# A two-layer decoder trunk on one core: chunk 2 of the SwiGLU FFN in seven block products, and norm steps issued ahead of weight splits

## The chip, the core and the metric

The kernel runs on one core of one Trainium2 chip. The time is device microseconds of one execution. Before the change it is 641.0 us, the median of 3 runs (639.06 to 641.35 us). One further execution was taken with the hardware profiler on; all rows below come from that one.

## The reference

Two layers, each a token mixer and a SwiGLU FFN, both between RMSNorms, on x of 256 rows by 1024 columns, all in float32:

```
h = h + rmsnorm(mixer(rmsnorm(h, mix_pre_norm)), mix_post_norm)
f = (silu(n @ w_gate) * (n @ w_up)) @ w_down      # n = rmsnorm(h, ffn_pre_norm)
h = h + rmsnorm(f, ffn_post_norm)
```

The mixer projects n by w_in (1024 x 3088) into attention heads and gated-linear-attention heads, and its result goes through w_out (1024 x 1024). w_gate and w_up are 1024 x 2816 and w_down is 2816 x 1024. The change touches the FFN and the norms between mixer and FFN; the mixer's inside is as it was.

## The kernel before, in words

**Three products for one.** Each float32 operand is split into a high part (`hi`, rounded to the float32r type by a ScalarE copy) and a low part (`lo`, the difference, by a VectorE subtraction). A product is then three TensorE matmuls: hi by hi, hi by lo, lo by hi. Weights come from HBM in pieces of two 128-row tiles by 512 columns (128x1024 in the rows), so each piece costs one ScalarE copy (`wh<-...`) and one VectorE subtraction (`wl<-...`). `highs` (L417) issues the copies and `lows_` (L437) the subtractions, both strictly in the order of `queue`. The split pieces lie in a ring of NW = 8: piece i can be split only when the matmuls on piece i-8 are done for both halves of the rows (j = 0 and j = 1, 128 rows each).

**The FFN's chunks.** The 2816 hidden columns go in six chunks, five of 512 and one of 256 (`FF_CHUNKS`). A plain chunk multiplies both row halves by w_gate and w_up: 8 row tiles of weight, two matrices, two halves, three matmuls, 96 matmuls of 128x512, and 8 weight pieces. A chunk listed in `SEVEN` (L42) goes through `seven` (L1283) instead: the 2x2 block product (two row halves by {gate, up}, with the 1024 inner rows cut in two) is computed with seven block products in place of eight: 84 matmuls. Its seven weight blocks (`SNAMES`) are three loaded ones and four sums (v1 to v4) of loaded ones; each block is two pieces, so 14 copies, 14 subtractions, and 8 additions of 128x1024 on VectorE for the sums (`sums`, L375). The results are combined by five small 128x512 VectorE operations (`gate0`, `hidden`) where a plain chunk has two. After chunk c, `down` (L1350) multiplies chunk c-1 by its 512 rows of w_down: four weight pieces, 48 matmuls for both halves.

**Tiles and loads.** Plain pieces are loaded into a ring of four (`raw`, NRAW). A seven-product chunk takes five tiles of 1 MB out of NBIG = 8 (`b11`, `b12`, `v1`, `b22`, `b21`; v2 and v4 are formed in b11's place, v3 in b12's). From the start of the FFN to the end of chunk 4 two more of the eight hold the split sums of the activations. All loads are issued by SyncE in one order (`loader`, L355).

**The order of the work.** `Clock` (L108) is a planner that runs when the program is built: it keeps an estimated time for each engine and wakes tasks by it. PE's estimated time is "now". `lows_` issues a subtraction when VectorE's estimated end is less than 0.7 us ahead of now; `sums` issues an addition when VectorE is not ahead at all, or up to 0.7 us when its block is due within two pieces. Each engine then executes its instructions in that order, waiting at each for its inputs. A step of a norm waits for `soon(x)` (L252), the estimated time at which x is ready, and is issued then; weight splits issued before that stand in front of it.

**The norms.** `post_norm` (L673) squares and sums the two PSUM banks of a row half (`sq`, ScalarE), multiplies by the gain (`pn`, VectorE), forms the factor (`var` on VectorE, `rstd` on GpSimd), and adds to h. `pre_norm_ffn` (L592) squares h, scales it (`xn`), transposes it on PE (`tp_x`), scales by the gain column (`a`), and splits (`xh_x` on ScalarE, `xl_x` on VectorE). Chunk 1's first product (`b11`, in the bank `seven_a`) is the first user of that.

Of the kernel before, what the change touches and what calls it, by code (L numbers as in the profile page):

```python
# [38 lines left out]
NEG = -1e30  # L39
LEVELS = (16, 8, 4, 2, 1)  # L40
FF_CHUNKS = (512, 512, 512, 512, 512, 256)
SEVEN = (1, 3, 4)  # L42
SNAMES = ("b11", "b21", "v2", "v1", "v3", "b22", "v4")
NW = 8
NRAW = 4
# [6 lines left out]
UNITS1 = [("gqk", 0), ("aq", 0), ("gqk", 1), ("aq", 1)] + UNITS0[2:]  # L52
BANKS = {"mm": 2, "tp": 2, "ac": 4}
SEM = 0.2


class Engine:
# [50 lines left out]
class Clock:  # L108
# [40 lines left out]
    def note(self, eng, cost, ins, outs):  # L149
# [3 lines left out]
        for ap in ins:  # L153
            r = self.ready(ap)
            start = max(start, r if eng == "PE" and ap in outs else r + SEM)
        if eng == "DMA":
# [21 lines left out]
    def tile(self, pool, shape, dtype, tag, bufs, name):  # L178
# [3 lines left out]
        while len(slots) >= bufs:  # L182
            done = [t for t in slots if t not in self.open]
            if done:
                t = min(done, key=lambda t: self.last.get(t, 0.0))
                slots.remove(t)
                free = self.last.get(t, 0.0) + SEM
                yield free
# [8 lines left out]
    def close(self, *tiles):  # L197
        for t in tiles:
            self.open.discard(t.tensor.name)

    def after(self, new, old):

        self.free[new.tensor.name] = self.last.get(old.tensor.name, 0.0) + SEM

# [33 lines left out]
def trunk(ctx: ExitStack, tc: tile.TileContext, io: dict):  # L238
# [7 lines left out]
    ck = Clock(nc)  # L246
    pe, act, dve, pool, dma, close = ck.pe, ck.act, ck.dve, ck.pool, ck.dma, ck.close

    def at(*aps):
        return ck.ready(*aps) + 0.5  # L250

    def soon(*aps):  # L252

        return ck.ready(*aps)

    def bank(tag, name):
        t = yield from ck.tile(ps, [P, 512], F32, tag, BANKS[tag], name)
        ck.port[t.tensor.name] = ("", 0.0)
        return t

    def t2(name):
        return ck.tile(sb, [P, 512], F32, "t2", NT2, name)
# [4 lines left out]
    def small(name, n=1):  # L267
        return sb.tile([P, n], F32, tag="small", bufs=20, name=name)
# [18 lines left out]
    def add_seven(l, c, f0, fw, what="all"):  # L287

        blocks = {}
        for n, name in ((1, "w_gate"), (2, "w_up")):  # L290
            for k in range(2):
                blocks[f"b{k + 1}{n}"] = io[name][l][512 * k:512 * (k + 1), f0:f0 + fw]
        if what != "rest":
            forms[l, c] = {"tiles": {}, "ready": {}, "low": {}}
        for name in {"first": ("b11", "b21"), "rest": ("b12", "v1", "b22")}.get(
                what, ("b11", "b12", "v1", "b22", "b21")):
            loads.append((name, (l, c), blocks.get(name)))
        for name in {"first": SNAMES[:2], "rest": SNAMES[2:]}.get(what, SNAMES):
            for g in range(2):
                queue.append(((l, "seven", c, name), 2 * g, 2, fw, None))  # L300

    for l in range(L):
# [10 lines left out]
        for c, fw in enumerate(FF_CHUNKS):  # L313
            if c == 0:
                add_seven(l, 1, fw, FF_CHUNKS[1], "first")
            if c in SEVEN:
                add_seven(l, c, f0, fw, "all" if c > 1 else "rest")
# [210 lines left out]
    def load_gain(i):  # L528
        if i < len(gains):
            gtiles[i] = gain(gains[i], D, "gain", 1)  # L530


    def rstd_of(parts_, n):

        v = small("var", n)
        if len(parts_) == 1:
            dve.tensor_scalar(v, parts_[0], EPS, None, op0=ALU.add)
        else:
            dve.scalar_tensor_tensor(v, parts_[0], EPS, parts_[1], op0=ALU.add, op1=ALU.add)
        r = small("rstd", n)  # L540
        pool.tensor_tensor(r, v, nhalf[:, :n], op=ALU.pow)
        return r

    def transpose_pe(src, t0, m, tp):
        for i in range(m):
            pe.transpose(tp[:, i * P:(i + 1) * P], src[:, (t0 + i) * P:(t0 + i + 1) * P], ident)
        return tp.rearrange("p (k t) -> p k t", t=P)[:, :m, :]
# [44 lines left out]
    def pre_norm_ffn(j, out, l):  # L592


        ms = []
        for i in range(2):
            c = slice(i * 512, (i + 1) * 512)
            junk = yield from ck.tile(sb, [P, 512], BF16, "t2", NT2, "sq")
            yield soon(h[j][:, c])
            m = small("ms")  # L600
            act.activation(junk, h[j][:, c], AF.Square, scale=1.0 / 32.0, accum_out=m)
            close(junk)
            ms.append(m)
        yield soon(*ms)
        r = rstd_of(ms, 1)
        xs = []
        if j == 0:
            sums_of[l] = []
            for name, dtype in (("a", F32), ("sums_h", R32), ("sums_l", R32)):
                t = yield from ck.tile(sb, [P, 4, 512], dtype, "big", NBIG, name)  # L610
                sums_of[l].append(t)
        while len(sums_of[l]) < 3:
            yield ck.now() + 0.1
        a = sums_of[l][0]
        for i in range(2):
            c = slice(i * 512, (i + 1) * 512)
            x = yield from t2("xn")
            yield soon(r)
            act.activation(x, h[j][:, c], AF.Copy, scale=r)
            xs.append(x)  # L620
        xt = []
        for i in range(2):
            hi = yield from ck.tile(sb, [P, 4, P], R32, f"xt{j}", 6, "xh_x")
            lo = yield from ck.tile(sb, [P, 4, P], R32, f"xt{j}", 6, "xl_x")
            yield at(xs[i])
            tp = yield from bank("tp", "tp_x")
            tv = transpose_pe(xs[i], 0, 4, tp)
            close(xs[i])
            yield soon(tp)
            av = a[:, 2 * j + i, :]  # L630
            for k in range(4):
                g = 16 + 8 * l + 4 * i + k
                act.activation(av[:, k * P:(k + 1) * P], tv[:, k, :], AF.Copy, scale=gcol[:, g:g + 1])
            close(tp)
            yield soon(av)
            act.activation(hi.rearrange("p k t -> p (k t)"), av, AF.Copy)
            yield soon(hi)
            dve.tensor_tensor(lo.rearrange("p k t -> p (k t)"), av,
                              hi.rearrange("p k t -> p (k t)").bitcast(F32), op=ALU.subtract)
            xt += [(hi[:, k, :], lo[:, k, :]) for k in range(4)]  # L640
        out[j] = xt
        if j == 1:
            yield from sums_x(out, l)
# [29 lines left out]
    def post_norm(j, banks, gi, then):  # L673

        g = gtiles[gi]
        ms, ts = [], []

        def square(i):
            junk = yield from t2("sq")
            yield soon(banks[i])  # L680
            m = small("msh")
            act.activation(junk, banks[i], AF.Square, scale=1.0 / 32.0, accum_out=m)
            close(junk)
            ms.append(m)

        def gained(i):
            t = yield from t2("pn")
            yield ck.port[banks[i].tensor.name][1]
            dve.tensor_tensor(t, banks[i], g[:, i * 512:(i + 1) * 512], op=ALU.mult)
            close(banks[i])  # L690
            ts.append(t)

        yield from square(0)
        if ck.ready(banks[1]) <= ck.at["Act"]:
            yield from square(1)
            yield from gained(0)
        else:
            yield from gained(0)
            yield from square(1)
        yield soon(*ms)  # L700
        r = rstd_of(ms, 1)
        yield from gained(1)
        yield soon(r)
        for i, w in ((0, 512), (512, 256), (768, 256)) if j and then is None else ((0, 512), (512, 512)):
            c = slice(i, i + w)
            dve.scalar_tensor_tensor(h[j][:, c], ts[i // 512][:, i % 512:i % 512 + w], r, h[j][:, c],
                                     op0=ALU.mult, op1=ALU.add)
            if then is None:
                dma.dma_start(io["out"][0, j * P:(j + 1) * P, c], h[j][:, c])
        close(*ts)  # L710
        if j == 1:
            load_gain(gi + 1)
        if then is not None:
            yield from then


    def mixer(l, xin, xout):
# [482 lines left out]
        for j in range(2):  # L1200
            while mixed[j][4] is None:
                yield ck.now() + 0.2
            bk = []
            for i in range(2):
                o = yield from bank("ac", f"wo{i}")
                bk.append(o)
            for part, lo in (("wo_g", 4), ("wo_a", 0)):
                while mixed[j][lo] is None:
                    yield ck.now() + 0.2
                yield from project((l, part), mixed[j][lo:lo + 4], bk, first=(lo == 4),  # L1210
                                   last=(lo == 0))
                close_x(mixed[j][lo:lo + 4])
            go(post_norm(j, bk, gi, pre_norm_ffn(j, xout, l)))


    def ffn(l, xin, xout):
# [145 lines left out]
        for c in range(nch):  # L1362
            if c in SEVEN:
                seq = []
# [5 lines left out]
            for part, j in seq:  # L1370
                yield from part(c, j)
            if c == max(SEVEN):
                close(*xin[2]["tiles"])
# [30 lines left out]
    h = [const.tile([P, D], F32, name=f"h{j}") for j in range(2)]  # L1404
# [110 lines left out]
```

## Time and profile before

| what | value |
|---|---|
| median of 3 runs | 641.0 us (639.06 to 641.35) |
| the profiled execution's own time | 639.99 us |
| its span, first to last instruction | 638.2 us |
| mean granted TensorE clock | 0.989 of full |
| mean HBM read rate over the span | 170 GB/s |
| VectorE instructions / ScalarE instructions | 784 / 700 |

How to read it: a busy share is an average over stages with different limits, so what a stage is worth is read from the stage's own window. PE is TensorE's matmuls, PEld its weight loads, DVE is VectorE, ACT is ScalarE, POOL is GpSimd, SP is SyncE. The duration of a matmul is that of a pipeline, longer than the distance from one matmul to the next. All instructions are recorded on L77, the helper that issues them, so they are told apart by the names of their tiles.

In layer 0 the FFN runs from 135.7 us to 323 us (first and last of its matmuls), in layer 1 from 447.7 us to 631.5 us.

### The profile page before, as it was taken

The page shows a single profiled execution, that of the slowest core. Times are in us where ns is not written, and L with a number is a line of the kernel's source. Part 1 is how long each engine was busy: PE and PEld are TensorE (multiplying, and loading weights), DVE is VectorE, ACT ScalarE, POOL GpSimd, SP SyncE. Part 2 cuts the span into 40 slices and gives each one's busy share as a digit, 9 for nine tenths or more (in the row PEclk, how much of TensorE's full clock was granted, in tenths as well). Part 3 has the DMA queues.
Part 4 walks back from the last instruction along what each step waited for, and adds up shares of the span by engine and source line. Part 5 has one row for each costly group of instructions (what it writes and reads, how often), then busy time and mean ns, then how long its engine had stood idle before and what let it go on. Part 6 is the DMA issues. An engine that isn't in the chain of part 4 may idle for free.

```text
span 638.2 us, 10255 instructions
## 1 busy us (share of the span) xinstructions
PE 622.1 (97%) x3896; PEld 510.7 (80%) x3896; DVE 504.3 (79%) x784; ACT 412.6 (65%) x700; POOL 23.7 (4%) x41
## 2 busy tenths in 40 slices
PE   8999999989999999999999999999899999999995
PEld 7987778868888888879788777887788888888894
DVE  4899975579897899987588996557899778989743
ACT  6889855486946385656577797537966555838531
POOL 1000021000000000000010000110000000000000
PEclk9999999979999999999999999999899999999998
DMA  8965455156048946039474714840910895710811
GB/s 281 281 193 156 149 188 191 52 174 255 1 142 294 397 152 201 1 104 289 142 246 149 205 46 126 277 142 17 368 45 3 286 353 216 270 61 1 263 68 66
DMA packets 53108, 109.30 MB, mean 171 GB/s; under 512 B 5890, under 2 KB 10692, under 8 KB 53060
## 3 DMA queue, kind: packets, MB, share of 16 engines
q1 hardware_dynamic: 53060, 108.66, 51.4%
q8 instruction: 30, 0.49, 0.3%
q14 instruction: 18, 0.15, 0.1%
HBM read 107.60 MB, written 1.05 MB: 170 GB/s over the span
## 4 chain that ended last, share of the span: by engine, by line
PE 86%; DVE 5%; DMA 3%; ACT 3%; issue 2%; SPq 1%; POOLq 0%; DVEq 0%; ACTq 0%
PE dn L77 17%; PE seven_a L77 10%; PE gate_ps L77 8%; PE up_ps L77 8%; PE seven_b L77 7%; PE wo L77 4%; PE gr L77 4%; PE gqk L77 4%; PE ak L77 4%; PE gv L77 3%; PE av L77 3%; PE aq L77 3%; DVE wl L77 3%; ACT wh L77 2%; PE att_o L77 2%
## 5 line engine op out<-in xcount | busy, mean ns | idle before, releaser
L77 DVE TENSOR_TENSOR wl<-raw,wh 128x1024 fp32r<-128x1024 f32 (+1 forms) x124 | 150.3, 1221 | 32.4 <-ACT wh L77 31.6
L77 ACT ACTIVATE wh<-raw 128x1024 fp32r<-128x1024 f32 (+1 forms) x124 | 130.0, 1059 | 54.1 <-DMA raw<-w_gate 17.3
L77 ACT ACTIVATE wh<-b 128x1024 fp32r<-128x1024 f32 x72 | 75.0, 1058 | 38.2 <-PE up_ps L77 9.3
L77 DVE TENSOR_TENSOR wl<-b,wh 128x1024 fp32r<-128x1024 f32 x72 | 84.9, 1218 | 2.9 <-ACT wh L77 2.8
L77 PE MATMUL dn<-wh,xh_h 128*128 128x512 f32 x176 | 70.4, 400 | 0.0
L77 PE MATMUL dn<-wl,xh_h 128*128 128x512 f32 x176 | 69.5, 395 | 0.0
L77 PE MATMUL dn<-wh,xl_h 128*128 128x512 f32 x176 | 69.1, 393 | 0.0
L77 DVE TENSOR_TENSOR b<-b,b 128x1024 f32<-128x1024 f32 x36 | 42.7, 1217 | 0.0
L77 POOL TENSOR_TENSOR rstd<-var,nhalf 128x1 f32<-128x1 f32 (+1 forms) x24 | 21.2, 883 | 557.6 <-DVE var L77 557.5
L77 PEld LDWEIGHTS dn<-wl,xh_h 128*128 128x128 f32 x176 | 33.1, 188 | 8.2 <-DVE wl L77 1.4
L77 PEld LDWEIGHTS dn<-wh,xl_h 128*128 128x128 f32 x176 | 33.0, 188 | 7.4
L77 PEld LDWEIGHTS dn<-wh,xh_h 128*128 128x128 f32 x176 | 33.1, 188 | 7.0
L77 DVE SCALAR_TENSOR_TENSOR wl<-raw,gcol,wh 128x512 fp32r<-128x512 f32 (+1 forms) x48 | 34.4, 748 | 1.6 <-ACT wh L77 1.6
L77 ACT ACTIVATE wh<-raw,gcol 128x512 fp32r<-128x512 f32 (+1 forms) x48 | 32.4, 717 | 4.7 <-DMA raw<-w_in 3.3
L77 PE MATMUL gate_ps<-wh,xh_x 128*128 128x512 f32 (+1 forms) x96 | 34.9, 363 | 0.0
L77 PE MATMUL up_ps<-wh,xh_x 128*128 128x512 f32 (+1 forms) x96 | 34.3, 358 | 0.0
L77 PE MATMUL gate_ps<-wh,xl_x 128*128 128x512 f32 (+1 forms) x96 | 34.1, 356 | 0.0
L77 PE MATMUL gate_ps<-wl,xh_x 128*128 128x512 f32 (+1 forms) x96 | 34.1, 355 | 0.0
L77 PE MATMUL up_ps<-wh,xl_x 128*128 128x512 f32 (+1 forms) x96 | 34.1, 355 | 0.0
L77 PE MATMUL up_ps<-wl,xh_x 128*128 128x512 f32 (+1 forms) x96 | 34.1, 355 | 0.0
L77 ACT ACTIVATE xh_h<-tp_h 128x512 fp32r<-128x512 f32 (+1 forms) x24 | 13.3, 554 | 25.1 <-PE tp_h L77 24.9
L77 DVE TENSOR_TENSOR xl_h<-tp_h,xh_h 128x512 fp32r<-128x512 f32 (+1 forms) x24 | 15.5, 645 | 14.9 <-ACT xh_h L77 14.8
(233 smaller groups left out, 1483.9 us busy)
## 6 DMA issues: line engine op xcount, KB each, us to landing
raw<-w_in SPq DMA_DIRECT2D x45, 512.0 KB, 4.6
raw<-w_down SPq DMA_DIRECT2D x44, 512.0 KB, 4.9
b<-w_gate SPq DMA_DIRECT2D x24, 512.0 KB, 8.2
b<-w_up SPq DMA_DIRECT2D x24, 512.0 KB, 7.5
raw<-w_gate SPq DMA_DIRECT2D x20, 512.0 KB, 4.4
raw<-w_up SPq DMA_DIRECT2D x20, 512.0 KB, 4.8
raw<-w_out SPq DMA_DIRECT2D x16, 512.0 KB, 3.7
raw<-w_in SPq DMA_DIRECT2D x6, 256.0 KB, 5.1
```

The source lines that it names most:

```text
L77: return f(*args, **kw)
```

## The change

`SEVEN` becomes (1, 2, 3, 4): chunk 2 of each layer goes through `seven` as well, with its sums on VectorE as the others have them. A new helper `next_` gives the estimated time of an input less LEAD = 1.1 us; the steps of `post_norm` and `pre_norm_ffn` wait for it in place of `soon`, so that they are issued up to 1.1 us of the planner's time earlier, in front of weight splits that would be issued in that time. In `pre_norm_ffn` the copy to `hi` is issued straight behind the four scalings. The activation sums (`sums_x`), the row factor of the mixer's pre-norm and `transpose_split` stay as they were.

```
-SEVEN = (1, 3, 4)
+SEVEN = (1, 2, 3, 4)
+LEAD = 1.1
+    def next_(*aps):
+        return ck.ready(*aps) - LEAD
 # pre_norm_ffn
-            yield soon(h[j][:, c])
+            yield next_(h[j][:, c])
-        yield soon(*ms)
+        yield next_(*ms)
-            yield soon(r)
+            yield next_(r)
-            yield soon(tp)
+            yield next_(tp)
             ...
             close(tp)
-            yield soon(av)
             act.activation(hi.rearrange("p k t -> p (k t)"), av, AF.Copy)
-            yield soon(hi)
+            yield next_(hi)
 # post_norm
-            yield soon(banks[i])
+            yield next_(banks[i])
-            yield ck.port[banks[i].tensor.name][1]
+            yield ck.port[banks[i].tensor.name][1] - LEAD
-        yield soon(*ms)
+        yield next_(*ms)
-        yield soon(r)
+        yield next_(r, *ts)
```

## Rows read from the trace of the kernel before

**Rows 1.** The page's first part: busy time, share of the span, instructions.
```profile
PE 622.1 (97%) x3896; PEld 510.7 (80%) x3896; DVE 504.3 (79%) x784; ACT 412.6 (65%) x700; POOL 23.7 (4%) x41
```

**Rows 2.** Windows: length, then busy us (instructions) by engine, PEclk, DMA share, GB/s.
```profile
124.90:180.50 55.60, 53.08 (x230) 42.62 (x228) 48.95 (x57) 44.69 (x74) 1.65 (x3) 0.94 0.36 123
180.50:277.60 97.10, 97.10 (x434) 79.02 (x433) 85.32 (x84) 58.86 (x66) 0.00 (x0) 1.00 0.56 195
437.00:491.40 54.40, 51.86 (x230) 41.77 (x229) 48.63 (x56) 44.65 (x74) 1.65 (x3) 0.97 0.35 126
491.40:588.40 97.00, 97.00 (x434) 78.93 (x433) 85.25 (x83) 58.73 (x66) 0.00 (x0) 1.00 0.56 195
```

**Rows 3.** Timeline of DVE in layer 0's FFN: start us, us, instruction, count.
```profile
165.87 1.29 DVE L77 TENSOR_TENSOR sums_l<-a,sums_h 128x512 fp32r<-128x512 f32 x2
...
178.21 2.35 DVE L77 TENSOR_TENSOR wl<-b,wh 128x1024 fp32r<-128x1024 f32 x2
...
256.49 4.62 DVE L77 TENSOR_TENSOR b<-b,b 128x1024 f32<-128x1024 f32 x4
...
275.27 2.35 DVE L77 TENSOR_TENSOR wl<-b,wh 128x1024 fp32r<-128x1024 f32 x2
```

**Rows 4.** Timeline of ACT: the copies behind the last products of chunks 1 and 4.
```profile
183.00 0.60 ACT L77 ACTIVATE sg<-seven_a 128x512 f32<-128x512 f32 x1 [4.44 <-PE seven_a L77]
...
279.95 0.60 ACT L77 ACTIVATE sg<-seven_a 128x512 f32<-128x512 f32 x1 [2.96 <-PE seven_a L77]
```

**Rows 5.** The chain of waits, chunk 2's up matmuls: start us, us, what.
```profile
206.13 11.09 PE up_ps L77 x48
```

**Rows 6.** Groups by form: the block sums of both layers' chunks 1, 3, 4.
```profile
L77 DVE TENSOR_TENSOR b<-b,b 128x1024 f32<-128x1024 f32 x36 | 42.7, 1217 | 0.0
...
L77 DVE TENSOR_TENSOR v<-b,b 128x1024 f32<-128x1024 f32 x12 | 14.5, 1218 | 3.3 <-DMA b<-w_up 3.3
```

**Rows 7.** DVE's waits from 180.5 to 277.6 us: total us, times, longest.
```profile
DVE wl L77 <- ACT wh L77: 6.8, 11, 1.5
DVE xl_h L77 <- ACT xh_h L77: 3.0, 4, 1.1
DVE v L77 <- DMA b<-w_up: 1.6, 1, 1.6
```

**Rows 8.** Groups of DVE from 240.9 to 277.6 us, with the idle before them.
```profile
L77 DVE TENSOR_TENSOR wl<-b,wh 128x1024 fp32r<-128x1024 f32 x13 | 15.2, 1218 | 0.0
...
L77 DVE TENSOR_TENSOR xl_h<-tp_h,xh_h 128x512 fp32r<-128x512 f32 x2 | 1.4, 692 | 1.9 <-ACT xh_h L77 1.9
```

**Rows 9.** Timeline of PE at the FFN's start in both layers.
```profile
135.66 0.50 PE L77 MATMUL seven_a<-wh,xh_x 128*128 128x512 f32 x1 [1.85 <-ACT xh_x L77]
...
137.12 0.80 PE L77 MATMUL seven_a<-wh,xl_x 128*128 128x512 f32 x1 [0.67 <-DVE xl_x L77]
...
447.74 0.50 PE L77 MATMUL seven_a<-wh,xh_x 128*128 128x512 f32 x1 [1.82 <-ACT xh_x L77]
...
449.19 0.50 PE L77 MATMUL seven_a<-wh,xl_x 128*128 128x512 f32 x1 [0.72 <-DVE xl_x L77]
```

**Rows 10.** Windows behind those gaps; PEclk is the third number from the end.
```profile
137.10:143.00 5.90, 5.88 (x14) 4.62 (x15) 4.26 (x5) 4.00 (x10) 0.00 (x0) 0.50 0.88 244
...
450.20:454.00 3.80, 3.80 (x11) 2.96 (x10) 3.13 (x5) 2.80 (x6) 0.00 (x0) 0.55 0.92 315
```

**Rows 11.** Timeline of ACT ahead of layer 0's first FFN product.
```profile
126.87 1.99 ACT L77 ACTIVATE wh<-b 128x1024 fp32r<-128x1024 f32 x2
...
132.88 1.06 ACT L77 ACTIVATE wh<-raw 128x1024 fp32r<-128x1024 f32 x1
...
134.97 0.64 ACT L77 ACTIVATE xh_x<-a 128x512 fp32r<-128x512 f32 x1
```

**Rows 12.** The page's DMA issues: count, KB each, median us from issue to landing.
```profile
b<-w_gate SPq DMA_DIRECT2D x24, 512.0 KB, 8.2
```

**Rows 13.** Timeline of SP's queue: chunk 2's first loads before the change.
```profile
182.36 4.98 SPq L77 DMA_DIRECT2D raw<-w_gate  x4
```

## The prediction, made before the changed kernel ran

> **What bounds the kernel now.** I read the page's busy shares first: PE is busy for 97% of the span, DVE for 79% [rows 1]. That points at PE, and in the sense of the whole span it is right. But the change acts in one stage, so I read windows next. From the last weight split of chunk 1 to that of chunk 4 DVE works 85.3 of 97.1 us in layer 0 and 85.3 of 97.0 in layer 1 [rows 2]; it has 11.8 us of idle time there, and the reader is to see that this is the whole reserve the change can draw on. The ends of the window are the places where DVE is almost late. The two pieces of chunk 1's last block (v4) are split by 179.4 and 180.6 us, those of chunk 4 by 276.5 and 277.6 [rows 3]; ACT picks up the product's result at 183.0 and 279.95 [rows 4], and 12 matmuls of 0.231 us (48 in 11.09 [rows 5]) put its start at 180.2 and 277.2. So the split is ready 0.7 to 0.8 us before PE wants it, at both ends. PE is never idle in the window, yet it has no more than that in hand. Chunk 2 in plain form is what refills the reserve before 3 and 4: most of DVE's waits of the window are `wl` behind ACT's copy [rows 7], which in turn waits for loads.
>
> My theory: in a run of seven-product chunks DVE, not PE, sets the pace.
>
> **The change, part by part.** The profiled execution took 639.99 us (span 638.2, so 1.8 around it), 1.0 below the median of the three runs; the sum is made on 640.0.
>
> *PE's saving.* 96 matmuls become 84: 12 x 0.231 = 2.8 us for each layer, 5.5 in all, if PE sets the pace.
>
> *DVE's added work.* 48 block sums stand for the six seven-product chunks before [rows 6], 8 for each. Chunk 2 gains those 8, and 14 splits in place of 8, so 14 operations of 128x1024; and 5 small operations in place of 2. Back to back, four large ones take 4.62 us [rows 3], with 1.22 for a lone one [rows 6] a pitch of (4.62-1.22)/3 = 1.13; two small ones take 1.29, a pitch of 0.61. Per layer 14 x 1.13 + 3 x 0.61 = 17.7 us. In the window that makes 85.3 + 17.7 = 103.0 us of DVE work against 97.1 available before, or 94.3 after PE's saving. Even with not one wait DVE needs 5.9 us more than the window had. A little can come off: the 16 operations that stand behind a wait now [rows 7] are booked at 1.22 and would cost 1.13 in a row, 1.4 us less. That is the lower end, +4.5 us for a layer.
>
> *What waits remain.* Of the 11.8 us of idle time 6.8 stand behind ACT's copies and 1.6 behind a load [rows 7]: those I take as filled by the new work. The 3.0 us of `xl_h` behind `xh_h` are of another kind: the transposed hidden rows come through PE and ACT, and DVE waits in order. From 240.9 to 277.6, the only stretch in which DVE is saturated from end to end, they cost 1.9 us in one chunk and its down product [rows 8]. Three such stretches would make 5.7, the upper end: 103.0 + 5.7 = 108.7, +11.6 us. When DVE runs late, part of these waits goes, because ACT is done before DVE arrives. I take +9 us for a layer, in the middle and nearer to the measured saturated stretch than to none: +18 for both. It falls as PE idling for `wl` of v2 to v4 in chunks 2, 3 and 4, and no later stage gives it back.
>
> ACT gains 6 copies of 1.06 and 3 small ones, about 8 us, into a window in which it works 58.9 of 97.1 [rows 2]: hidden.
>
> *Loads.* The bytes are the same, but chunk 2 now loads into the large tiles, which come free as chunk 1's splits end. Two of eight hold the activation sums, so one tile is free early and four follow by the time that v4's splits begin, 178.2 [rows 3]. A load lands after 8.2 us [rows 12], at 186; v2 is wanted after 183.0 plus the down product and two block products (48 + 24 matmuls, 16.6 us), at 199.6. SP issues in order and its loads for chunk 2 started at 182.4 before [rows 13]; they now start earlier. I cost it at nothing; if the last tile were held until chunk 1's v4 ended, DVE's sums would still begin ahead of need.
>
> *The norms.* At the FFN's start PE idles 1.85 + 0.67 us in layer 0 and 1.82 + 0.72 in layer 1 [rows 9], and then runs with a granted clock of 0.50 and 0.55, close to the lower of its two levels, 1.2 GHz [rows 10]: 14 matmuls in 5.90 us where 0.231 each makes 3.2, and 11 in 3.80 where it makes 2.5. Together 2.5 + 2.7 and 2.5 + 1.3, 9.0 us for both layers. In the way stood ACT's weight copies: two of them from 126.87, one more at 132.88, and `xh_x` came only at 134.97 [rows 11]. Steps issued 1.1 us earlier pass these, so PE's gaps can go; what is late next is DVE. From 124.9 to 180.5 it works 48.9 of 55.6 [rows 2], and each step issued early now also stands at the head of its queue until its input comes, with splits behind it that PE will want. So chunk 1's end moves forward by what DVE can save of its 6.7 us (5.8 in layer 1), not by PE's gap. Bounds: 9.0 us gained in all, or 2 lost (1 a layer, for DVE standing at `var`, `pn` and h). I take half of the gap, 2.5 us a layer, -5. The steps at the mixer's start and at the program's end have no splits in front of them worth a microsecond; I take nothing.
>
> The Trainium skill, "TensorE: Matmul & The Clock Gate", Part 1, says that an array that has idled is clocked down and must be busy for a while to be clocked up; rows 10 agree. By that rule PE waits of the new kind, if they fall together in one place, would cost about 2 us more each time.
>
> Sum: 640.0 + 18 - 5 = 653.0 us.
>
> **The rivals.**
>
> *PE sets the pace, so fewer matmuls are faster (the other side).* For it: 97% against 79% [rows 1]. Against it: the windows. It decides from the point at which DVE's added work fits its idle time: it would need 17.7 us or more free in each window where there are 11.8. Time: 640.0 - 5.5 - 5 = 629.5. The Trainium skill, "Perfetto Trace Analysis", section "Identifying the Most-Contended Engine", says to take the engine of highest occupancy as the bottleneck and to better that one first; for TensorE it names the share of the weight loads. By that rule PE (80% by PEld) still stands a hair above DVE (79%), and the forecast would be this rival's; the windows disagree.
>
> *The norms pay for it.* The full 9.0 us come, and DVE packs its work without a wait: 640.0 + 2 x 5.9 - 9.0 = 642.8, no change that can be measured. For it: PE's gap is real and ACT's copies are visibly what fills it. Against it: both halves need DVE to run without idle time from the FFN's start to chunk 4's end, where it now idles for 6.7 and 11.8 us [rows 2].
>
> *The norms cost too.* Early steps hold DVE's queue for 1 us a layer, all `xl_h` waits stay: 640.0 + 2 x 11.6 + 2 = 665.2. For it: chunk 1's end has under 1 us in hand [rows 3, 4], and everything behind it shifts.
>
> **How the numbers follow.** My forecast 0.65; PE sets the pace 0.06; the norms pay 0.17; the norms cost 0.12. About 0.5% (3.2 us) is what a measurement can tell from no change. Faster by over that (below 637) is the first rival and a tail of the second: 0.07. Within it (637 to 643.2): most of the second and the edge of the forecast at its lower end: 0.11. Slower: 0.82. The forecast's own range is 640.0 + 2 x 4.5 - 5 = 644 to 640.0 + 2 x 11.6 - 2 = 661; the neighbours widen it to 642 and 665.
>
> **What would show it.** Right: in the chunks 2 to 4 of the changed kernel DVE is busy over 95% of its time, PE idles several microseconds in `seven_a` and `seven_b`, released by DVE `wl`, and the time from chunk 1's v4 to chunk 4's grows by 6 to 11 us in each layer; the gap at the FFN's first product shrinks or goes. Wrong: PE stays without a gap in chunks 2 to 4 (then DVE had more reserve than the windows show), or DVE is not saturated while PE waits (then it is the loads or ACT), or the gap at the FFN's start is as it was.

## The result and the profile after

The changed kernel takes 671.1 us (median of 4 runs, 668.6 to 674.6); the kernel before took 640.6 beside it (639.1 to 641.4). The ratio is 1.048, 95% interval 1.043 to 1.054. I had forecast 653.0 with a range of 642 to 665: slower was right, the size was not. The profiled execution took 668.6 us, its span is 666.8.

The page's first part, to be held against [rows 1]: PE has 24 matmuls less and is still busy 3.6 us longer, some of it at the lower clock; DVE works 33 us more, and the span grows by 28.6.

```profile
PE 625.7 (94%) x3872; PEld 508.5 (76%) x3872; DVE 537.1 (81%) x818; ACT 422.1 (63%) x718; POOL 26.0 (4%) x41
```

I cut both spans at the same four places of PE's timeline: the first product of chunk 1 (`b11`), the end of chunk 1's last block product (v4), the same end in chunk 4, and the next layer.

| stretch | layer 0, before and after | layer 1, before and after |
|---|---|---|
| mixer, up to `b11` | 135.7, 135.5 | 125.3, 123.8 |
| `b11` to the end of chunk 1's v4 | 47.1, 55.3 | 46.0, 55.2 |
| to the end of chunk 4's v4 | 97.0, 103.8 | 96.9, 103.9 |
| the rest | 42.7, 42.0 | 0.3 less |

The growth is 13.9 us in the window that I had costed for DVE, and 17.4 us in a stretch from which I had expected a gain. Layer 1's mixer stretch is 1.4 shorter because the gap at its end is gone; in layer 0 the mixer ran later in this execution, at a lower clock (0.92 from 80 to 102 us, where it was 1.00 before).

Windows of the changed kernel, with the columns of [rows 2]: from chunk 1's v4 to chunk 4's in layer 0, then three stretches for the clock.

```profile
190.72:294.56 103.84, 97.17 (x422) 77.38 (x420) 101.93 (x101) 59.96 (x72) 0.00 (x0) 0.98 0.42 142
152.30:160.00 7.70, 4.31 (x10) 3.22 (x11) 7.60 (x11) 5.54 (x9) 0.00 (x0) 0.56 0.35 110
196.10:199.50 3.40, 3.34 (x10) 2.69 (x11) 3.40 (x5) 0.00 (x0) 0.00 (x0) 0.69 0.59 171
231.60:235.00 3.40, 3.32 (x14) 2.70 (x15) 3.40 (x5) 0.00 (x0) 0.00 (x0) 1.00 0.63 196
```

In the first line DVE is busy for 101.9 of 103.8 us (85.3 of 97.1 in [rows 2]): it sets the pace there. Its busy time alone is 5 us more than the whole stretch took before. The waits of that window, PE's and then DVE's (total us, times, longest), and PE's three long ones:

```profile
PE dn L78 <- DVE wl L78: 6.1, 3, 2.3
PE seven_b L78 <- DVE wl L78: 0.6, 3, 0.2
```

```profile
DVE xl_h L78 <- ACT xh_h L78: 1.7, 1, 1.7
```

```profile
196.16 0.50 PE L78 MATMUL dn<-wl,xh_h 128*128 128x512 f32 x1 [2.29 <-DVE wl L78]
231.68 0.50 PE L78 MATMUL dn<-wl,xh_h 128*128 128x512 f32 x1 [1.93 <-DVE wl L78]
265.68 0.50 PE L78 MATMUL dn<-wl,xh_h 128*128 128x512 f32 x1 [1.89 <-DVE wl L78]
```

PE waits for splits of DVE, as forecast, but once in each down product and hardly in v2 to v4. DVE's own timeline says why: two sums stand in front of the last two pieces of w_down, and PE wants those pieces first (the same two rows stand in front of the other two waits, at 227.5 and 261.5).

```profile
192.01 1.22 DVE L78 TENSOR_TENSOR v<-b,b 128x1024 f32<-128x1024 f32 x1
...
193.75 1.22 DVE L78 TENSOR_TENSOR v<-b,b 128x1024 f32<-128x1024 f32 x1
194.89 2.35 DVE L78 TENSOR_TENSOR wl<-raw,wh 128x1024 fp32r<-128x1024 f32 x2
```

Now the stretch that surprised. PE's timeline from the FFN's first product, against [rows 9]:

```profile
135.46 0.39 PE L78 MATMUL seven_a<-wh,xh_x 128*128 128x512 f32 x1
...
141.04 0.50 PE L78 MATMUL seven_b<-wl,xh_x 128*128 128x512 f32 x1 [1.03 <-DVE wl L78]
...
152.37 0.50 PE L78 MATMUL gate_ps<-wh,xh_x 128*128 128x512 f32 x1 [3.58 <-ACT wh L78]
156.19 0.79 PE L78 MATMUL gate_ps<-wl,xh_x 128*128 128x512 f32 x1 [3.32 <-DVE wl L78]
```

The gap at the first product is gone: no idle time, and the twelve matmuls take 2.8 us where they took 5.9. But at the last weight piece of chunk 0's gate, two products later, PE waits 3.58 us for the copy and 3.32 for the subtraction, and the granted clock of that stretch is 0.56, near the lower level. Gate's 24 matmuls take 16.2 us in place of 6.0. Layer 1 shows the same: 3.58 and 3.03 us at gate, and 2.24, 1.91 and 1.93 us in the down products. ACT's timeline shows what the copy of the weights waited for:

```profile
137.38 1.06 ACT L78 ACTIVATE wh<-raw 128x1024 fp32r<-128x1024 f32 x1
...
140.57 1.04 ACT L78 ACTIVATE wh<-raw 128x1024 fp32r<-128x1024 f32 x1
143.77 1.34 ACT L78 ACTIVATE xn<-h,rstd 128x512 f32<-128x512 f32 x2 [2.15 <-POOL rstd L78]
145.01 1.04 ACT L78 ACTIVATE wh<-raw 128x1024 fp32r<-128x1024 f32 x1
145.96 1.12 ACT L78 ACTIVATE a<-tp_x,gcol 128x128 f32<-128x128 f32 x4
147.11 0.63 ACT L78 ACTIVATE xh_x<-a 128x512 fp32r<-128x512 f32 x1
147.76 1.28 ACT L78 ACT_TABLE_LOAD   x1
149.05 0.63 ACT L78 ACTIVATE p<-p 128x512 f32<-128x512 f32 x1
149.59 1.13 ACT L78 ACTIVATE a<-tp_x,gcol 128x128 f32<-128x128 f32 x4
150.75 0.63 ACT L78 ACTIVATE xh_x<-a 128x512 fp32r<-128x512 f32 x1
151.28 3.88 ACT L78 ACTIVATE wh<-raw 128x1024 fp32r<-128x1024 f32 x4
```

The same stretch before the change, the weight copies and the table load alone (one more copy, at 132.88, is in [rows 11]):

```profile
129.99 1.99 ACT L77 ACTIVATE wh<-raw 128x1024 fp32r<-128x1024 f32 x2
...
135.49 1.07 ACT L77 ACTIVATE wh<-raw 128x1024 fp32r<-128x1024 f32 x1
...
139.24 1.06 ACT L77 ACTIVATE wh<-raw 128x1024 fp32r<-128x1024 f32 x1 [0.98 <-PE seven_a L77]
...
142.90 2.00 ACT L77 ACTIVATE wh<-raw 128x1024 fp32r<-128x1024 f32 x2
...
146.02 1.05 ACT L77 ACTIVATE wh<-raw 128x1024 fp32r<-128x1024 f32 x1
147.09 1.28 ACT L77 ACT_TABLE_LOAD   x1
```

Before, all eight pieces of chunk 0's gate and up were copied ahead of the table load; now three are. Four copies that used to be spread between the steps of the norm stand together behind all of them, the second row half's chain included. DVE in turn stands idle for 2.94 us ahead of `xl_x` and subtracts the pieces from 154.92. A second thing is in the same rows: ACT waited 2.15 us for `rstd`, the 128x1 factor on GpSimd. Its row in the changed kernel:

```profile
141.20 2.54 POOL L78 TENSOR_TENSOR rstd<-var,nhalf 128x1 f32<-128x1 f32 x1 [2.80 <-DVE var L78]
```

The same row of the kernel before:

```profile
143.34 0.55 POOL L77 TENSOR_TENSOR rstd<-var,nhalf 128x1 f32<-128x1 f32 x1 [6.77 <-DVE var L77]
```

### The profile page after: what moved, and what is told of

Its sections match the earlier page's. It is cut to its first block, busy times and chain, and to the rows that moved or that the text cites. A ratio compares the mean times of both kernels' runs of the same rounds, so it can differ in the third digit from the quotient of the medians.

```text
span 666.8 us, 10235 instructions
## 1 busy us (share of the span) xinstructions
PE 625.7 (94%) x3872; PEld 508.5 (76%) x3872; DVE 537.1 (81%) x818; ACT 422.1 (63%) x718; POOL 26.0 (4%) x41
## 4 chain that ended last, share of the span: by engine, by line
PE 61%; DVE 26%; ACT 5%; issue 4%; POOL 1%; DMA 1%; DVEq 0%; SPq 0%; POOLq 0%; ACTq 0%
DVE wl L78 13%; PE dn L78 12%; DVE b L78 6%; PE wo L78 5%; PE up_ps L78 5%; PE gate_ps L78 4%; PE gr L78 4%; PE ak L78 4%; PE gqk L78 4%; PE av L78 4%; PE aq L78 3%; PE gv L78 3%; PE seven_a L78 2%; PE seven_b L78 2%; PE att_o L78 2%
## 5 line engine op out<-in xcount | busy, mean ns | idle before, releaser
L78 DVE TENSOR_TENSOR wl<-raw,wh 128x1024 fp32r<-128x1024 f32 (+1 forms) x108 | 129.8, 1220 | 24.2 <-ACT wh L78 23.9
L78 ACT ACTIVATE wh<-raw 128x1024 fp32r<-128x1024 f32 (+1 forms) x108 | 110.6, 1057 | 33.6 <-DMA raw<-w_gate 8.3
L78 DVE TENSOR_TENSOR wl<-b,wh 128x1024 fp32r<-128x1024 f32 x96 | 112.7, 1219 | 4.2 <-ACT wh L78 4.2
L78 ACT ACTIVATE wh<-b 128x1024 fp32r<-128x1024 f32 x96 | 96.0, 1052 | 2.5 <-PE wo L78 1.3
L78 DVE TENSOR_TENSOR b<-b,b 128x1024 f32<-128x1024 f32 x48 | 56.6, 1218 | 0.0
L78 PE MATMUL seven_b<-wl,sums_h 128*128 128x512 f32 x64 | 25.7, 402 | 1.1 <-DVE wl L78 1.1
L78 PE MATMUL seven_a<-wh,xh_x 128*128 128x512 f32 x64 | 25.7, 402 | 0.0
L78 PE MATMUL seven_b<-wh,sums_h 128*128 128x512 f32 x64 | 25.3, 395 | 0.0
L78 PE MATMUL seven_a<-wl,xh_x 128*128 128x512 f32 x64 | 25.1, 393 | 0.0
L78 PE MATMUL seven_b<-wh,sums_l 128*128 128x512 f32 x64 | 25.1, 393 | 0.0
```

Source lines behind the costliest of these rows:

```text
L78: return f(*args, **kw)
```

## The experiments

Theory: two separate costs. **Sums:** in chunks 2 to 4 DVE has no time for eight more sums and six more splits. **Lock-out:** `highs` and `lows_` issue a split only while the planner's estimated end of their engine is within 0.3 (ACT) or 0.7 us (DVE) of now; a norm step that may be issued 1.1 us ahead pushes that end beyond the limit, and by the time now has caught up the next step of the norm is due. So a chain of early steps shuts the splits out altogether. The rivals come with each run. The lists of PE's waits below are for 135 to 260 us, layer 0's FFN but for its end.

**e1: seven products alone.** In the kernel before:

```
-SEVEN = (1, 3, 4)
+SEVEN = (1, 2, 3, 4)
```

> The kernel before with chunk 2 in seven products and the norms left as they were. Theory (two separate costs: DVE sets the pace in chunks 2 to 4, and the early norm steps hold back gate's weight pieces in chunk 0): chunk 1's first product to its v4 as before (47.1 and 46.0 us), from chunk 1's v4 to chunk 4's 103.8 us in place of 96.9 in each layer, so 640.6 + 2 x 6.9 = 654. Rival (the costs are one: DVE enters chunk 2 late because the norms made chunk 1 late, so without the early steps the reserve suffices): 640.6 - 5.5 to 645.

Measured 652.2 us, ratio 1.018 [1.014, 1.021]: +11.2. The gap at the first product stays, and behind it only the down products wait for long, as in the changed kernel. From chunk 1's v4 to chunk 4's it takes 105.3 us in layer 0 and 102.2 in layer 1, DVE being busy for 101.9 in both. PE's waits, then a window over most of that stretch:

```profile
PE dn L77 <- DVE wl L77: 6.0, 3, 2.1
```

```profile
180.50:286.00 105.50, 98.93 (x422) 78.66 (x422) 102.03 (x101) 61.91 (x74) 0.00 (x0) 0.97 0.41 140
```

**e2: the norm edits alone**, in the changed kernel:

```
-SEVEN = (1, 2, 3, 4)
+SEVEN = (1, 3, 4)
```

> The change's norm steps alone, chunk 2 plain as before. Theory (two separate costs): the gap in front of the FFN's first product goes, but gate of chunk 0 waits some 7 us for its fourth weight piece in each layer and then runs at the lower clock; chunk 1's first product to v4's end 55 us in place of 46 to 47, less 2 us for the gap; 640.6 + 2 x 6.7 = 654. Rival (the lateness of chunk 1 comes from chunk 2's loads or sums, which chunk 1's DVE work meets early): 631 to 638, the gain that the prediction counted on.

Measured 657.4 us, 1.026 [1.022, 1.029]: +16.3. Chunks 2 to 4 are without a wait; the stretch from `b11` to chunk 1's v4 has 56.0 us. The two costs add up to 27.5 of the 30.5 us; the 3 us left over are within the intervals of the three runs, 2 to 3 us to either side each. PE's waits:

```profile
PE gate_ps L78 <- ACT wh L78: 3.6, 1, 3.6
PE gate_ps L78 <- DVE wl L78: 3.0, 1, 3.0
PE seven_b L78 <- DVE wl L78: 1.0, 1, 1.0
```

**e4: fewer sums.** e1 without chunk 2's sums for v2, v3 and v4:

```
-                for g in range(2):
+                for g in range(0 if c == 2 and name != "v1" else 2):
```

> As the run with chunk 2 in seven products alone, but chunk 2's sums v2, v3 and v4 are left out (their blocks are split as loaded); 6 of 8 additions, 6.8 us of DVE a layer. Theory (DVE's work sets the pace): the added work falls from 17.7 to 10.9 us, under the 11.8 that were idle, so PE sets the pace again: 96 to 98 us from chunk 1's v4 to chunk 4's, 638 to 643. Rival (chunk 2 waits for its loads, its tiles or the ring of split pieces): as slow as with the sums, 652 to 656.

Measured 646.4 us, 1.008 [1.005, 1.012]. Half of the loss went, less than I expected. From chunk 1's v4 to chunk 4's it takes 100.8 us in both layers with DVE busy for 95.2, so DVE has 5.6 us of idle time and PE waits all the same. Two of the three waits stay, since the two sums of v1 still stand in front of the pieces of w_down there (chunk 2's own v1, which this run keeps, and chunk 4's). Here it is the order that costs.

```profile
PE dn L77 <- DVE wl L77: 4.2, 2, 2.1
```

**e6: another order.** e1, with sums let ahead later:

```
-  ... (AHEAD[1] if due - len(parts) <= 2 else 0.0):
+  ... (AHEAD[1] if due - len(parts) <= 0 else 0.0):
```

> Chunk 2 in seven products, norms as before, and a block sum goes ahead of other splits only when its own block is the next to be split (in place of two pieces before). Theory (DVE's work sets the pace; the order only says where PE waits): the waits leave the down products and come up in front of v2, chunk 1's v4 to chunk 4's still 101 to 105 us, 649 to 655. Rival (the order alone costs it: sums issued in front of down's pieces hold PE for 2 us a chunk): the waits go, 97 us or less, 637 to 642.

Measured 656.2 us, 1.024 [1.021, 1.027], 1 us above the expected range. The waits left the down products and came up in the block products (a third, of 1.52, at 272.9):

```profile
PE seven_a L77 <- DVE wl L77: 3.0, 2, 1.5
```

From v4 to v4 it takes 104.5 and 104.4 us, DVE being busy for 100.9. With all eight sums in place it is DVE's throughput, and the order only chooses where PE waits.

**e7: chunk 2's sums on GpSimd**, in e1 (the planner counts 2.2 us for one):

```
+                    if c == 2:
+                        pool.tensor_tensor(*v, op=ALU.add)
+                        continue
```

> Chunk 2 in seven products, norms as before, chunk 2's eight sums on GpSimd in place of DVE, which leaves DVE 8.6 us of added work a layer for 11.8 us of idle time. Theory (DVE's work sets the pace): most of the loss goes; what stays is the wait at the down product behind chunk 2 that the run with few sums had (2 us and a lower clock behind it): 637 to 646. Rival (loads, tiles or the ring): 650 to 655. If GpSimd's sums take over 3 us each they come late themselves, and v2 of chunk 2 waits: over 655.

Measured 668.8 us, 1.044 [1.040, 1.048]: worse than with the sums on DVE. PE's long waits of chunks 1 and 2 are at chunk 1's v4 (2.6 in all), in the down product (3.9) and at chunk 2's v1 (3.2), each for DVE. Groups of the stretch from 185 to 215 us, where GpSimd adds (count, then busy us and mean ns):

```profile
L77 POOL TENSOR_TENSOR b<-b,b 128x1024 f32<-128x1024 f32 x6 | 19.9, 3342 | 8.2 <-DVE wl L77 8.2
L77 DVE TENSOR_TENSOR wl<-b,wh 128x1024 fp32r<-128x1024 f32 x8 | 15.4, 1961 | 0.0
L77 DVE TENSOR_TENSOR wl<-v,wh 128x1024 fp32r<-128x1024 f32 x2 | 6.3, 3127 | 0.0
```

The first DVE form takes 1218 ns in [rows 8]. GpSimd needs 3.3 us for a sum, and DVE is slowed beside it: from v4 to v4 of layer 0 it is busy for 105.0 us, with chunk 2's sums gone from it, where e1 has 101.9. The eight sums were not taken off DVE so much as paid for by its other work.

**e3: early steps for the first row half only.** e2, where `next_` gives no lead for j = 1, and the wait before the copy to `hi` stands again there:

```
-            yield next_(tp)
+            yield next_(j, tp)
 ...
+            if j:
+                yield soon(av)
```

> The early steps for the first row half only (j = 0); the second half issues its steps as before, chunk 2 plain. Theory (what hurts is that the second half's steps, each issued 1.1 us early, lock gate's and up's weight copies out of ACT): the first gap goes as in the changed kernel and gate of chunk 0 waits under 2 us; 632 to 638. Rival (ACT simply has too much to do there, whichever half comes first): gate still waits 5 us or more, 648 to 655.

Measured 653.8 us, 1.019 [1.016, 1.023]. My expectation of a full recovery failed. Gate's wait falls to 0.4 us, and up, the next product, waits instead:

```profile
PE up_ps L78 <- DVE wl L78: 6.2, 2, 5.9
PE gate_ps L78 <- DVE wl L78: 0.4, 1, 0.4
```

**e5: splits let in.** e2, with one rule added to `highs` and `lows_`: while a norm is under way they may reach 1.1 us further ahead too (ACT's lines, like DVE's, and the count in `norms` are left out here).

```
+    def ahead(i):
+        return AHEAD[i] + (LEAD if norms[0] else 0.0)
 ...
-                while ck.at["DVE"] > ck.now() + AHEAD[1]:
+                while ck.at["DVE"] > ck.now() + ahead(1):
```

> The change's norm steps with chunk 2 plain; while a norm is under way the planner may issue weight splits up to 1.1 us further ahead, so an early step no longer shuts them out. Theory A (lock-out: an early step puts the planner's end time of ACT beyond its limit, and no split is issued until now has caught up): gate's wait of 7.3 us in chunk 0 goes or falls under 1 us, and up's stays under 2; 636 to 644. Theory B (ACT and DVE have as much to do there as the time before the changed start of PE allows; the gap that PE had in front of the FFN was time the splits needed): the wait only moves on to up's last pieces, 4 us or more a layer, 646 to 656.

Measured 643.4 us, 1.004 [1.000, 1.008]: 14 of 16.3 us come back. In this order the second half's factor on GpSimd takes 0.55 us again (2.54 in e2), so a part of the 14 is the factor's; e15 prices that. Gate has no wait; up keeps one, longer than the 2 us that I expected at most:

```profile
PE up_ps L78 <- DVE wl L78: 3.1, 1, 3.1
```

**e10: e3 with e6's rule for the sums.**

> Chunk 2 plain, early norm steps for the first row half only, and a block sum goes ahead only when its own block is the next to be split. In the run with the first half alone, up's last piece was copied by ACT at 153.8 us but split by DVE at 159.9, behind two sums and the activation sums. Theory A' (it is the order on DVE, two sums and an activation step in front of up's last piece, that makes up wait 6.2 us): that piece now stands ahead of them, up waits under 2 us, 634 to 643. Theory B (ACT and DVE are short of time there whatever the order): chunk 1 comes later by as much somewhere else, 647 to 655.

Measured 646.3 us, 1.008 [1.006, 1.010], between the theories: up waits 1.1, a transposition of the hidden rows (`tp_h`) waits 1.6 for DVE, and 2.0 moved to v2 and v4.

**e8: no lead.** e2 with `LEAD = 0.0`, so that of the norm edits the missing wait in front of the copy to `hi` is left, and that `post_norm`'s last step waits for `ts` too.

> The norm edits with a lead of 0 in place of 1.1 us: the steps are issued as early as before, and only the wait in front of the copy to the high part of the rows is gone. Theory (the lead makes the lock-out): with no lead norm steps never push the planner's end beyond what splits may reach, so the gate's wait of 7 us a layer goes and the time is 638 to 645, the gap at the first product being about as before. Rival (the order of the copy to the high part is what delays the splits): the gate's or up's wait stays at over 4 us a layer and the time is 650 or above.

Measured 647.4 us, 1.009 [1.006, 1.013], between the two again: gate has no wait (the lead made that one), but up waits 3.8 us, so that the place of this copy very likely costs something by itself. And the gap at the first product is gone here too, in both layers, against my expectation:

```profile
135.49 0.50 PE L78 MATMUL seven_a<-wh,xh_x 128*128 128x512 f32 x1
```

So the copy's place is enough to close the gap; it does not take the lead. The copy's place with the splits let in and no lead was not run.

**e12: e3 and e5 together**: early steps for the first row half, splits let in.

> The kernel before with early norm steps for the first row half only (as in e3), and splits let in 1.1 us further ahead while a norm is under way (as in e5). Theory A, the lock-out is the only cost of early steps: the gap of 2.5 us at the first product goes, no wait takes its place, 634 to 639. Theory B, from the first product to the end of chunk 1 DVE's work has no room for an earlier start, so that what PE gains at the first product it waits for at up or in v4: 639 to 646, with up and v4 waits that add to 2 to 4 us in each layer. From e5 and e10 I hold B for likelier.

Measured 638.7 us (10 runs) against 642.1, 0.996 [0.992, 0.999]: the best version of the study, in the range of theory A where I had held B for likelier. PE's first product has no gap in front, and `b11` to v4 takes 47.4 and 45.9 us, as long as before the change. One wait of over 0.5 us is left, in layer 0's chunk 1, at v1:

```profile
174.51 0.50 PE L78 MATMUL seven_b<-wl,sums_h 128*128 128x512 f32 x1 [1.92 <-DVE wl L78]
```

**e14: only the splits let in**, in the kernel before.

> The kernel before with e12's second rule alone: splits let in 1.1 us further ahead while a norm is under way, and no norm step issued earlier. It tells whether e12's small gain is of early steps and the rule together. If it takes both: the gap at the first product of chunk 1 stays at 2.5 us or grows, since more splits stand in front of the norm's steps, and the time is that of before or more, 640 to 648. If the rule alone gives the gain: 636 to 640, with the gap as before and no wait anywhere in chunk 1.

Measured 646.7 us, 1.008 [1.006, 1.010]. The gap at the first product grows, from the 1.85 and 0.67 of [rows 9] to:

```profile
138.71 0.79 PE L78 MATMUL seven_a<-wh,xh_x 128*128 128x512 f32 x1 [3.45 <-ACT xh_x L78]
...
140.74 0.80 PE L78 MATMUL seven_a<-wh,xl_x 128*128 128x512 f32 x1 [0.80 <-DVE xl_x L78]
```

So each rule alone loses, early steps for the first half 13 us and splits let in 5; together they gain 3.

**e13: the changed kernel with the splits let in.**

> The changed kernel, with one rule added: while a norm is under way, weight splits too may be issued 1.1 us further ahead (as in e5). My theory, two separate costs: block sums that DVE has no time for (measured alone: +11) and splits locked out by early norm steps (measured alone: +16; with this rule +2). Then the time is that of before + 11 + 2, 651 to 657, and the wait at the gate's low pieces in layer 0 (3.3 us in the changed kernel) goes, while the waits in chunk 1's and 2's down products (about 2 us each) stay. Rival: in the full change the lock-out is not what costs at the gate, because chunk 2's early sums fill DVE there; then the time stays at 665 or above.

Measured 658.8 us, 1.029 [1.025, 1.033], 2 us above the expected range. Gate's waits are gone, and the down products' stay (the third, of 1.93, is at 261.8), with up's as in e5: letting the splits in gave 12 us of the change back. Of what stays, 7.0 and 6.9 us lie between chunk 1's v4 and chunk 4's, DVE's part; `b11` to chunk 1's v4 is 2.5 and 3.6 us longer than before, as in e5 (2.3 and 3.6), for up's wait.

```profile
PE dn L78 <- DVE wl L78: 4.2, 2, 2.3
PE up_ps L78 <- DVE wl L78: 3.1, 1, 3.1
```

**e15: the factor taken off GpSimd.** e2 with each engine's order kept, and the 128x1 factor of the FFN's pre-norm formed by DVE; a multiplication stands in for the power. The planner still books 0.55 us on GpSimd for it, which keeps the orders.

```
+            ck.note("Pool", 0.55, [v, nhalf[:, :n]], [r])
+            eng.tensor_tensor(r, v, nhalf[:, :n], op=ALU.mult)
 ...
-        r = rstd_of(ms, 1)
+        r = rstd_of(ms, 1, nc.vector)
```

> The norm edits alone (as e2), every engine's order as in e2, but the four 128x1 factors of the FFN's pre-norm are formed on DVE, right behind their sum, by a multiplication in place of the power on GpSimd (so the rows' scale is wrong; its duration is what is asked). In e2 the second of them took 2.54 to 2.60 us on GpSimd, with two 128x1024 splits of DVE beside it, and ACT waited 2.15 us for it with the weight copies queued behind. Theory C, that lengthening is a large part of the gate's wait: ACT's wait at xn and 2 us of the gate's 6.6 us of wait a layer go, 651 to 655 (e2: 657.4). Theory A, the lock-out alone: the last copies stand behind the second half's chain whatever the factor does, the gate's wait stays over 6 us a layer, 656 to 659. If the lengthening is all of it, the time is 645 or under.

Measured 654.6 us, 1.020 [1.013, 1.026], where e2 had 657.4. The stretch from `b11` to v4 is 53.8 us in layer 0 (56.0 in e2) and 54.0 in layer 1 (55.3). DVE's new row, and the two waits that stay:

```profile
142.83 0.16 DVE L550 TENSOR_TENSOR rstd<-var,nhalf 128x1 f32<-128x1 f32 x1
```

```profile
152.52 0.50 PE L78 MATMUL gate_ps<-wh,xh_x 128*128 128x512 f32 x1 [3.25 <-ACT wh L78]
156.34 0.80 PE L78 MATMUL gate_ps<-wl,xh_x 128*128 128x512 f32 x1 [3.32 <-DVE wl L78]
```

By the traces the long factor costs 2.2 of the 8.9 us that e2 adds to this stretch in layer 0, where e2's clock was also the lower (0.91 against 0.94), and 1.3 of 9.3 in layer 1, where the clocks were equal. In layer 0 gate's two waits add up to 6.6 us, as in e2; they end 1.6 us earlier behind `b11` in both layers. The rest is there with all orders as in e2, so it is the order. The intervals of the two runs' times overlap, and the factor's price rests on the two traces alone.

**e16 and e17: the same edit in e12 and in the kernel before.**

> e12 with the same edit (the power left out, a multiplication on DVE in its place). In e12 three of the four factors took 1.40 to 1.47 us in place of 0.55. Theory C: the FFN's first product starts about 1 us earlier in each layer and the waits at v2 do not grow, 635 to 638 where e12 had 638.7. Theory A or a DVE-bound chunk 1: what starts earlier waits later, 638 to 641.

> Control: the kernel before with the same edit. Its four factors took 0.55 us each, without a split beside them, so nothing but 0.4 us of each can come: 639 to 642 by both theories. A gain of over 3 us would say that GpSimd's factor costs something the trace does not show.

Measured 640.7 us, 0.999 [0.997, 1.002], and 641.7 us, 1.000 [0.998, 1.002]. (In e12's trace all four factors took 1.40 to 1.47 us, not three, and its wait is at v1.) The control is as it should be. e16 gains nothing on e12 and is itself not to be told from the kernel before, so e12's 0.4% is at the edge of what can be measured.

## Why the prediction was wrong

**The norms: the failed step.** "I take half of the gap, 2.5 us a layer, -5", with a loss of at most "1 a layer, for DVE standing at `var`, `pn` and h". Measured alone, the edits cost 16.3 us (e2). The gain itself was real: the gap of [rows 9] and the slow matmuls of [rows 10] are gone, though e8 shows that the place of the copy to `hi` is enough for that, without the 1.1 us that I had credited with it (before the change one weight copy and the other half's two squares, from 132.88 to 135.09, stand on ACT between the scalings and that copy). What I missed is the other side of a fixed budget. I treated the early steps as passing a few weight copies, and costed the time for which a step stands at the head of a queue. In fact the copies were not passed but shut out: in ACT's timelines three of chunk 0's eight pieces are copied ahead of the table load where all eight were before, and the next four come in one block, for which PE is already standing. I had taken the limit from DVE's idle time over the whole stretch from 124.9 to 180.5; it was nearer, at the fourth and last piece that gate needs. e5 shows it by one rule that gives 14 us back, e14 that the rule does nothing good alone. The lead made about 11 of the 16.3 us; with none, e8 still lost 5.3. A smaller part of the loss, 1.3 to 2.2 us a layer by e15's traces, is the factor on GpSimd, which nothing in my working mentions.

**DVE's added work: right, and a little large.** I took +9 us a layer, between 4.5 and 11.6; the window grew by 6.9 and 7.0. Both terms were a little large: the busy time is 101.9 against my 103.0, and the idle time that stays 1.9 against the 3.1 of my middle. I had allowed for up to three times 1.9 at `xl_h`, and one wait of 1.7 is left. DVE at over 95% of its time was right (98%), and so was that no later stage gives anything back beyond 0.7 us. As a whole the term gave 11.2 us alone (e1), against 18.

**Where PE waits: wrong.** I said v2 to v4; it is the down product (6.1 of 6.7 us). With all sums in place the total is set by DVE's work, and the place by the planner's order, as e6 shows by moving it. e4 adds that the order costs by itself where DVE does have time.

**The clock after a wait.** I had forecast some 2 us more for each place where waits fall together. After gate's pair of waits the clock is 0.56, and the first down product, at 0.69 behind its wait of 2.29, takes 15.6 us where the next two take 13.7: 1.9 more. But behind the waits of 1.93 and 1.89 the clock stays at 1.00. In e1 a wait of 1.91 was followed by 0.50 (product 15.3 us), and one of 2.12 by 1.00 (13.9), so the length of the single wait does not decide. The Trainium skill, "TensorE: Matmul & The Clock Gate", Part 1, says that an idle array is clocked down; the changed kernel's trace agrees at gate and at one down product of three in each layer.

**Loads and ACT: right.** No load ends a wait of DVE in the window, and ACT works 60.0 of 103.8 us.

**The rivals.** "PE sets the pace" falls with e1, where PE has 12 matmuls less in each layer and the kernel is slower. "The norms cost too" had the right sign and the wrong mechanism: its price was 2 us. "The norms pay for it" was near in how tightly DVE packs its work (1.9 us of idle time left) and wrong in the norms' sign.

## What to carry to other kernels

Read the reserve of a stage from its own window: an engine at 79% over the span had 12 us to spare where 18 were added. Where a planner lets one kind of work run ahead of a common budget, ask which other work that budget then refuses, and when its consumer wants it; give both kinds the same lead, or neither. Where one edit does two things, as the lead and the copy's place here, run each alone. A gap that disappears proves nothing until the next products have been read too.

## What the runs showed of the hardware

GpSimd and DVE hold each other up. The 128x1 factor takes 0.55 us on GpSimd when DVE pauses or multiplies out of PSUM (`pn`), and 1.40 to 1.54 beside one 128x1024 subtraction of two operands. Beside two or three in a row it is either that or 2.53 to 2.60; in the changed kernel it ended 0.4 us behind the second of a pair (143.74, DVE's pair at 143.32). In e7 it went the other way: means of 1.96 and 3.13 us for DVE's 1.22. The Trainium skill, "GPSIMD Engine Reference", section "Specifications", says that the two share their paths to SBUF and contend when DVE's instruction has two operands there; both traces agree. The same page's "Engine selection" calls two-operand work about twice as slow on GpSimd as on VectorE; here, with DVE working beside it, it was 2.4 to 2.8 times (2.89 and 3.44 us for sums of v and b, over all of e7).
